# Compact 32x32 squares for the lower doublings of the delta chunks' inverse, and attention by tasks of both key heads in halves of the array

## The chip, the core and the metric

The kernel runs on one core of a Trainium2 chip. A core has a matrix engine (TensorE, PE in the rows, with PEld its weight loads), a vector engine (VectorE, DVE), a scalar engine (ScalarE, ACT), a general engine (GpSimd, POOL), and DMA queues, of which SyncE (SP) issues most. Each engine works through its own instructions in a fixed order and waits on semaphores for the others. The metric is the device time of one execution in microseconds (us), the median of several runs; lower is better.

## What is computed

Two transformer blocks over 1024 tokens of width 1024. The change lies in the mixers of the first block: attention with 8 query heads, 2 key heads of 64 wide and a sliding window of 128, and a gated delta rule with 4 heads of 128 wide in chunks.

```python
s = jnp.einsum('bnqhgd,bnkhd->bnhgqk', qb, kw) * scale     # block of 128 queries against itself and the block before
s = jnp.where(valid, s, -jnp.inf)
probs = softmax(concatenate([s, sink], -1))[..., :-1]
o = jnp.einsum('bnhgqk,bnkhd->bnqhgd', probs, vw)
...
L = where(strict, einsum('bhncd,bhnsd->bhncs', k_beta, k) * decay, 0.0)
T = triangular_solve(eye + L, eye, lower=True)             # the inverse that the doublings make
u = einsum('bhncs,bhnsd->bhncd', T, v_beta)
w = einsum('bhncs,bhnsd->bhncd', T, k_beta * exp(g)[..., None])
...                                                        # scan over chunks, then norm and gate
h = h + concatenate([attn_out, dn_out], -1) @ w_o
h = h + square(relu(rmsnorm(h) @ w_up)) @ w_down           # and a gate; then the second block
```

## The kernel before, in words

Tokens stand in two halves of 512 columns (`H`), features in tiles of 128 partitions. Projections are dense products of 128x128 weights with 512 columns, each as three products of split high and low parts (`acc`, L211 to L213); they take most of the time.

Between about 137 and 600 us of the profile `weave` interleaves three lanes of tasks with these dense products (`fills`). Its tasks are first attention, then the delta heads. Each round steps every live lane once (to its next `yield`) and adds `rate()` to a counter that releases one dense step (24 products) for each whole: `RA` at first, `RB` from `FA` finished attention tasks on, `R1` when all are done. Lane 0 takes only the first `FA` attention tasks and then starts on a delta head; the other lanes begin delta heads when all attention tasks are done. A scheduler then fixes the order on each engine from this program; the order doesn't change at run time. Each lane owns two PSUM tiles (`axps`, tags x0 to x2) and one SBUF tile for each role a to g, with two `tmp`.

Attention (`attn`) has 16 tasks, one for a block of 128 queries and one key head. A key head's 64 features lie in one half of the partitions, so its score products (L649, L651) use 64 rows of the array, and its value products (L679) write 64 columns. A task does two steps (`jj`) of two query heads: scores, mask (L654), softmax, transposes (L673), a copy of them (L675), values. The output tile `po` is taken at the start of the task and holds both steps until ACT copies it (L682).

A delta head (`delta`; 4 heads and 2 halves give 8 tasks) makes four 128x128 chunks at once and inverts the unit lower triangle of each by doublings: from a level's inverted blocks of side b the level makes blocks of side 2b. Levels 1 to 4 work on whole 128x128 matrices: `L` times the odd columns of `X` (L782), mask (L785), a DVE transpose of `X` within 32x32 blocks (L784), a second product (L789), subtraction (L790). Levels 5 and 6 already use squares of 32 and 64 (L807, L815). All products here are fp32, and the trace shows each product of this kind as two records, each with a weight load; the transposes by the array and the dense products are one record.

Of the kernel before, what the change touches and what calls it, by code (L numbers as in the profile page):

```python
# [19 lines left out]
NC = S // 128  # L20
# [33 lines left out]
RA, RB, R1, R5 = 0.1, 0.2, 0.35, 0.9  # L54
FA, POOL_AT = 10, 2
# [6 lines left out]
def block_kernel(ctx: ExitStack, tc: tile.TileContext, A):  # L62
# [12 lines left out]
    const.tile([128, 64], F32, name="pad")  # L75
# [82 lines left out]
    def mask(l):  # L158

        a = cst("masks")[:, l * 64:(l + 1) * 64].rearrange("p (n b) -> p n b", b=1 << l)  # L160
        return a.unsqueeze(1).to_broadcast([128, 4, 64 >> l, 1 << l])

# [357 lines left out]


# [112 lines left out]
    def attn(lane, qr, kr, vT, n, kv):  # L634
# [4 lines left out]
        r = slice(kv * 64, kv * 64 + 64)  # L639
        am = cst("amask")[:, 256 - w:256].unsqueeze(1).to_broadcast([128, 2, w])  # L640
        po = axps(lane)
        for jj in range(2):
            ps = axps(lane)
            p3 = ps[:, :2 * w].rearrange("p (j k) -> p j k", j=2)
            for i in range(2):
                q = qr[2 * jj + i][n // 4][r, cs(n % 4)]
                if n % 4 == 0:
                    for b, m in enumerate(blocks):
                        PE.matmul(p3[:, i, cs(b)], q, kr[m // 4][r, cs(m % 4)], start=True, stop=True)  # L649
                else:  # L650
# [5 lines left out]
            m, nm, den, s2 = sm(2, "am"), sm(2, "an"), sm(2, "ad"), sm(2, "as")  # L656
            sk = small("sinks", kv * 4 + 2 * jj, 2)
            V.tensor_reduce(m, e3, AX.X, ALU.max)
            V.tensor_tensor(m, m, sk, ALU.max)
            V.tensor_scalar(nm, m, -1.0, None, ALU.mult)  # L660
            for i in range(2):
                SC.activation(e3[:, i], e3[:, i], ACTF.Exp, bias=nm[:, i:i + 1], accum_out=s2[:, i:i + 1])
            V.tensor_tensor(den, sk, m, ALU.subtract)
# [3 lines left out]
            for i in range(2):  # L667
                V.tensor_scalar(e3[:, i], e3[:, i], den[:, i:i + 1], None, ALU.mult)
            yield
            pp = axps(lane)  # L670
            for q in range(nb):
                for i in range(2):
# [50 lines left out]
    def delta(lane, j, h, y, z):  # L723
# [697 lines left out]
```

## Time and profile before

| | |
|---|---|
| median of 3 runs | 2673.6 us |
| lowest and highest | 2668.96 and 2673.8 us |
| the profiled execution | 2670.03 us |
| its span, first to last instruction | 2667.9 us |
| PE busy | 2570.0 us, 96% of the span |
| DVE, ACT, POOL busy | 67%, 36%, 13% |

The profile is one execution. Its views give the busy time of each engine, in all and by stretch, groups of instructions of one line and shape, the engines' instructions in order of time, who waited for whom, and the chain of work that ended last. A matmul's duration includes its passage through the array and overlaps with the next, so what one costs PE is read from the distance between starts.

### The profile page before, as it was taken

The numbers are of one execution on the slowest core, as the hardware profiler recorded it, in microseconds if no ns is written. First come the engines' busy times: TensorE is split into PE (matmuls) and PEld (weight loads), VectorE is DVE, ScalarE is ACT, GpSimd is POOL, SyncE is SP. The second block draws the span as 40 slices with busy tenths as digits, with TensorE's granted clock in tenths as the row PEclk, the third lists the DMA queues.
The fourth block names the chain that finished last, engine by engine and source line by source line (L and its number), as shares of the span: only waits on it lengthen the run. The fifth ranks groups of instructions, "written<-read, shape, count | busy, mean of one in ns | idle before, by whom it ended". The sixth has DMA issues, their size and how long they took to land.

```text
span 2667.9 us, 34945 instructions
## 1 busy us (share of the span) xinstructions
PE 2570.0 (96%) x12814; PEld 2081.7 (78%) x12814; DVE 1794.8 (67%) x3289; ACT 971.1 (36%) x1568; POOL 356.9 (13%) x398
## 2 busy tenths in 40 slices
PE   6999999999899999999999999999988999999997
PEld 4766787877688888878877888888867888888886
DVE  8777789878987765465457643446589876654653
ACT  4477533314322245344333322222133222444441
POOL 5511112110000000000022343333200000000000
PEclk8999999999999999999999999999989999999998
DMA  5312111245644366445422411113455433665652
GB/s 199 95 52 68 41 37 52 94 148 183 206 157 133 127 229 227 166 152 196 151 78 69 160 56 40 44 34 105 152 181 191 155 131 131 214 210 195 220 195 77
DMA packets 161675, 357.00 MB, mean 134 GB/s; under 512 B 18272, under 2 KB 22752, under 8 KB 161504
## 3 DMA queue, kind: packets, MB, share of 16 engines
q1 hardware_dynamic: 156080, 345.84, 38.5%
q10 hardware_dynamic: 5424, 8.94, 1.0%
q8 instruction: 100, 1.64, 0.3%
q14 instruction: 71, 0.58, 0.1%
HBM read 282.35 MB, written 69.73 MB: 132 GB/s over the span
## 4 chain that ended last, share of the span: by engine, by line
PE 83%; DVE 9%; issue 4%; POOL 2%; DMA 1%; ACT 1%; POOLq 0%; SPq 0%; DVEq 0%; ACTq 0%
PE m L212 13%; PE m L213 13%; PE m L211 13%; PE x L213 10%; PE x L212 10%; PE x L211 10%; PE x L1196 1%; PE x L679 1%; PE x L789 1%; PE x L782 1%; DVE wl L192 1%; PE x L651 1%; DVE u L192 1%; PE x L1202 1%; PE x L673 1%
## 5 line engine op out<-in xcount | busy, mean ns | idle before, releaser
L211 PE MATMUL m<-u,wh 128*128 128x512 f32 x1668 | 671.8, 403 | 11.0 <-ACT wh L191 6.8
L213 PE MATMUL m<-u,wl 128*128 128x512 f32 x1668 | 665.4, 399 | 11.1 <-DVE wl L192 11.1
L212 PE MATMUL m<-u,wh 128*128 128x512 f32 x1668 | 666.9, 400 | 2.4 <-DVE u L192 1.2
L192 DVE TENSOR_TENSOR wl<-wr,wh 128x1024 fp32r<-128x1024 f32 (+2 forms) x265 | 328.0, 1238 | 296.5 <-ACT wh L191 283.0
L191 ACT CAST wh<-wr 128x1024 fp32r<-128x1024 f32 (+2 forms) x265 | 276.0, 1041 | 548.0 <-PE m L212 335.5
L213 PE MATMUL x<-u,wl 128*128 128x512 f32 x1020 | 397.9, 391 | 6.4 <-DVE wl L192 6.4
L212 PE MATMUL x<-u,wh 128*128 128x512 f32 x1020 | 398.5, 391 | 4.1 <-DVE u L192 4.1
L211 PE MATMUL x<-u,wh 128*128 128x512 f32 x1020 | 398.6, 392 | 2.4 <-ACT u L191 2.2
L211 PEld LDWEIGHTS m<-u,wh 128*128 128x128 f32 x1668 | 317.2, 190 | 80.7 <-ACT wh L191 7.3
L213 PEld LDWEIGHTS m<-u,wl 128*128 128x128 f32 x1668 | 317.2, 190 | 79.6 <-DVE wl L192 13.3
L212 PEld LDWEIGHTS m<-u,wh 128*128 128x128 f32 x1668 | 317.3, 190 | 73.6 <-issue 6.6
L213 PEld LDWEIGHTS x<-u,wl 128*128 128x128 f32 x1020 | 192.3, 189 | 47.6 <-DVE wl L192 7.7
L212 PEld LDWEIGHTS x<-u,wh 128*128 128x128 f32 x1020 | 192.1, 188 | 45.9 <-DVE u L192 5.4
L211 PEld LDWEIGHTS x<-u,wh 128*128 128x128 f32 x1020 | 192.2, 188 | 44.9 <-ACT u L191 3.5
L191 ACT CAST u<-f 128x512 fp32r<-128x512 f32 x198 | 122.1, 620 | 187.6 <-PE x L212 73.8
L192 DVE TENSOR_TENSOR u<-f,u 128x512 fp32r<-128x512 f32 x174 | 123.4, 709 | 95.0 <-PE x L212 50.9
L191 ACT CAST wh<-y 128x512 fp32r<-128x512 f32 x91 | 55.1, 621 | 218.9 <-PE x L212 131.3
L192 POOL TENSOR_TENSOR u<-f,u 128x512 fp32r<-128x512 f32 x24 | 35.6, 1481 | 609.2 <-ACT u L191 608.4
L192 DVE TENSOR_TENSOR u<-r,u 128x512 fp32r<-128x512 f32 x128 | 88.1, 688 | 5.8 <-ACT u L191 5.8
L191 ACT CAST u<-r 128x512 fp32r<-128x512 f32 x128 | 79.2, 619 | 11.6 <-DMA r<-hid 8.8
L192 DVE TENSOR_TENSOR wl<-y,wh 128x512 fp32r<-128x512 f32 x91 | 61.7, 682 | 0.0
L248 DVE TENSOR_TENSOR ac<-ac,sq 128x512 f32<-128x512 f32 x70 | 53.7, 767 | 9.5 <-ACT sq L247 8.7
(742 smaller groups left out, 3714.1 us busy)
## 6 DMA issues: line engine op xcount, KB each, us to landing
wr<-in_w_down SPq DMA_DIRECT2D x128, 512.0 KB, 4.0
wr<-in_w_in SPq DMA_DIRECT2D x75, 512.0 KB, 3.2
r<-hid SPq DMA_DIRECT2D x128, 256.0 KB, 4.0
f<-hid SPq DMA_DIRECT2D x128, 256.0 KB, 3.3
y<-in_w_up SPq DMA_DIRECT2D x85, 256.0 KB, 3.2
hid<-f SPq DMA_DIRECT2D x52, 256.0 KB, 2.0
wr<-in_w_up SPq DMA_DIRECT2D x20, 512.0 KB, 4.0
hid<-sq SPq DMA_DIRECT2D x32, 256.0 KB, 3.1
```

Source lines behind the costliest of these rows:

```text
L191: SC.copy(hi, src)
L192: eng.tensor_tensor(lo, src, hi.bitcast(F32), ALU.subtract)
L211: PE.matmul(ps, whi[:, s], xh, start=(first and k == 0), stop=False)
L212: PE.matmul(ps, whi[:, s], xl, start=False, stop=False)
L213: PE.matmul(ps, wlo[:, s], xh, start=False, stop=(last and k == len(x) - 1))
L248: V.tensor_tensor(a, a, sq, ALU.add)
L651: PE.matmul(p3[:, i], q, kr[n // 4][r, (n % 4 - 1) * 128:(n % 4 + 1) * 128], start=True, stop=True)
L673: PE.transpose(pp[:, cs(2 * q + i)], e3[:, i, cs(q)], ident)
L679: PE.matmul(po[r, jj * 256:jj * 256 + 256], vT[m // 4][:, b:b + 64], pT[:, q * 256:q * 256 + 256], start=(q == 0), stop=(q == nb - 1))
L782: PE.matmul(py[:, c * 64:c * 64 + 64], L[:, cs(c)], odd(X[:, cs(c)], l), start=True, stop=True)
L789: PE.matmul(pz[:, c * 64:c * 64 + 64], T[:, cs(c)], Y[:, c * 64:c * 64 + 64], start=True, stop=True)
L1196: PE.matmul(ps[:, c * 64:c * 64 + 64], k[:, cs(c)], odd(q[:, cs(c)], l), start=True, stop=True)
```

## The change

Delta heads: for levels 1 to 4 only the four 32x32 squares on the diagonal of each chunk are kept, side by side in a tile of 128 columns (`Xc`: partitions 32i to 32i+31 hold square i of all four chunks). A step is 16 products of one square with 16 columns (L817 and L824 of the new file, in place of L782 and L789), going round the four squares. The DVE operations on them have 128 or 64 columns in place of 512 or 256. The masks are made compact once at the start, by eight POOL copies. After level 4, POOL clears the full `X` and ACT copies the squares into it; level 5 reads the compact ones.

Attention: 8 tasks, one for each block of queries, with both key heads. A step takes two score tiles, one for each key head, and issues their products in turn on rows 0 to 63 and 64 to 127; the value products go in turn to the two column halves of one tile, which is now taken at the end of the step and copied and sent at once. `FA` goes from 10 of 16 tasks to 5 of 8, and `RA` and `RB` are doubled.

```diff
-RA, RB, R1, R5 = 0.1, 0.2, 0.35, 0.9
-FA, POOL_AT = 10, 2
+RA, RB, R1, R5 = 0.2, 0.4, 0.35, 0.9
+FA, POOL_AT = 5, 2
...
+    def dg(i):
+        return slice(32 * i, 32 * i + 32)
+
+    def cmask(l):
+        t = cmask4 if l == 4 else cmasks[:, l * 16:l * 16 + 16]
+        return t.unsqueeze(1).to_broadcast([128, 4, 16])
+
+    def cmasks_in():
+        for i in range(4):
+            m = cst("masks")[dg(i), :].rearrange("p (l n) -> p l n", l=5)[:, :, 16 * i:16 * i + 16]
+            G.tensor_copy(cmasks[dg(i), :].rearrange("p (l n) -> p l n", l=4), m[:, 0:4])
+            G.tensor_copy(cmask4[dg(i), :], m[:, 4])
...
+    cmasks_in()
...
-        r = slice(kv * 64, kv * 64 + 64)
+        rs = [slice(0, 64), slice(64, 128)]
         am = cst("amask")[:, 256 - w:256].unsqueeze(1).to_broadcast([128, 2, w])
-        po = axps(lane)
         for jj in range(2):
-            ps = axps(lane)
-            p3 = ps[:, :2 * w].rearrange("p (j k) -> p j k", j=2)
+            ps = [axps(lane), axps(lane)]
+            p3 = [p[:, :2 * w].rearrange("p (j k) -> p j k", j=2) for p in ps]
             for i in range(2):
-                q = qr[2 * jj + i][n // 4][r, cs(n % 4)]
+                q = qr[2 * jj + i][n // 4]
                 if n % 4 == 0:
                     for b, m in enumerate(blocks):
-                        PE.matmul(p3[:, i, cs(b)], q, kr[m // 4][r, cs(m % 4)], start=True, stop=True)
+                        for kv, r in enumerate(rs):
+                            PE.matmul(p3[kv][:, i, cs(b)], q[r, cs(n % 4)], kr[m // 4][r, cs(m % 4)], start=True, stop=True)
                 else:
-                    PE.matmul(p3[:, i], q, kr[n // 4][r, (n % 4 - 1) * 128:(n % 4 + 1) * 128], start=True, stop=True)
-            e = td("ab"[jj], lane)
-            e3 = e[:, :2 * w].rearrange("p (j k) -> p j k", j=2)
-            V.tensor_tensor(e3, p3, am, ALU.add)
+                    for kv, r in enumerate(rs):
+                        PE.matmul(p3[kv][:, i], q[r, cs(n % 4)], kr[n // 4][r, (n % 4 - 1) * 128:(n % 4 + 1) * 128], start=True, stop=True)
+            es = [td("ab"[kv], lane)[:, :2 * w].rearrange("p (j k) -> p j k", j=2) for kv in range(2)]
+            for kv in range(2):
+                V.tensor_tensor(es[kv], p3[kv], am, ALU.add)
             yield
...
+            for kv in range(2):
+                V.tensor_reduce(two(m, kv), es[kv], AX.X, ALU.max)
+            V.tensor_tensor(d2(m), d2(m), sk, ALU.max)
             V.tensor_scalar(nm, m, -1.0, None, ALU.mult)
...
+            for kv in range(2):
+                for i in range(2):
+                    k = 2 * kv + i
+                    SC.activation(es[kv][:, i], es[kv][:, i], ACTF.Exp, bias=nm[:, k:k + 1], accum_out=s2[:, k:k + 1])
...
-            for i in range(2):
-                V.tensor_scalar(e3[:, i], e3[:, i], den[:, i:i + 1], None, ALU.mult)
+            for kv in range(2):
+                V.tensor_tensor(es[kv], es[kv], two(den, kv).unsqueeze(2).to_broadcast([128, 2, w]), ALU.mult)
             yield
-            pp = axps(lane)
-            for q in range(nb):
-                for i in range(2):
-                    PE.transpose(pp[:, cs(2 * q + i)], e3[:, i, cs(q)], ident)
-            pT = td("tmp", lane)
-            SC.copy(pT[:, :2 * w], pp[:, :2 * w])
+            pT = []
+            for kv in range(2):
+                pp = axps(lane)
+                for q in range(nb):
+                    for i in range(2):
+                        PE.transpose(pp[:, cs(2 * q + i)], es[kv][:, i, cs(q)], ident)
+                t = td("tmp", lane)
+                SC.copy(t[:, :2 * w], pp[:, :2 * w])
+                pT.append(t)
             yield
+            po = axps(lane)
             for q, m in enumerate(blocks):
-                b = (m % 4) * 128 + kv * 64
-                PE.matmul(po[r, jj * 256:jj * 256 + 256], vT[m // 4][:, b:b + 64],
-                          pT[:, q * 256:q * 256 + 256], start=(q == 0), stop=(q == nb - 1))
-        f = td("tmp", lane)
-        SC.copy(f[r, :], po[r, :])
+                for kv, r in enumerate(rs):
+                    b = (m % 4) * 128 + kv * 64
+                    PE.matmul(po[r, 0:256], vT[m // 4][:, b:b + 64], pT[kv][:, q * 256:q * 256 + 256],
+                              start=(q == 0), stop=(q == nb - 1))
+            f = td("tmp", lane)[:, 0:256]
+            SC.copy(f, po[:, 0:256])
+            nc.sync.dma_start(
+                out=mix["d"][256 * jj:256 * jj + 256, cs(n)].rearrange("(i q) t -> q i t", q=128),
+                in_=f.rearrange("p (i t) -> p i t", i=2),
+            )
...
-        nc.sync.dma_start(
-            out=mix["d"][0:512, cs(n)].rearrange("(i q) t -> q i t", q=128)[r],
-            in_=f[r, :].rearrange("p (i t) -> p i t", i=4),
-        )
...
-        X = td("d", lane)
-        Y = td("a", lane)
-        G.tensor_copy(g4(X), b4(ident))
-        V.tensor_tensor(half4(Y, 0), odd(U, 0, 4), mask(0), ALU.mult)
-        V.tensor_tensor(odd(X, 0, 4), odd(X, 0, 4), half4(Y, 0), ALU.subtract)
...
+        Xc, Y = td("g", lane)[:, 0:128], td("a", lane)[:, 0:64]
+        y4 = lambda t: t[:, 0:64].rearrange("p (c n) -> p c n", c=4)
+        for i in range(4):
+            G.tensor_copy(Xc[dg(i), :].rearrange("p (c n) -> p c n", c=4), ident[dg(i), dg(i)].unsqueeze(1).to_broadcast([32, 4, 32]))
+        for i in range(4):
+            V.tensor_tensor(y4(Y)[dg(i)], g4(U)[dg(i), :, 32 * i + 1:32 * i + 32:2], cmask(0)[dg(i)], ALU.mult)
+        V.tensor_tensor(odd(Xc, 0), odd(Xc, 0), Y.unsqueeze(2), ALU.subtract)
         yield
+        blocks = [(c, dg(i), slice(c * 128 + 32 * i, c * 128 + 32 * i + 32), slice(c * 16, c * 16 + 16)) for c in range(4) for i in range(4)]
         for l in range(1, 5):
             py = axps(lane)
-            for c in range(4):
-                PE.matmul(py[:, c * 64:c * 64 + 64], L[:, cs(c)], odd(X[:, cs(c)], l), start=True, stop=True)
-            Y, T = td("a", lane), td("b", lane)
-            V.transpose(T, X)
-            V.tensor_tensor(half4(Y, l), half4(py, l), mask(l), ALU.mult)
+            for c, p, m, n in blocks:
+                PE.matmul(py[p, n], L[p, m], odd(Xc[p, dg(c)], l), start=True, stop=True)
+            Y, T = td("a", lane)[:, 0:64], td("b", lane)[:, 0:128]
+            V.transpose(T, Xc)
+            V.tensor_tensor(y4(Y), y4(py), cmask(l), ALU.mult)
             yield
             pz = axps(lane)
-            for c in range(4):
-                PE.matmul(pz[:, c * 64:c * 64 + 64], T[:, cs(c)], Y[:, c * 64:c * 64 + 64], start=True, stop=True)
-            V.tensor_tensor(odd(X, l, 4), odd(X, l, 4), half4(pz, l), ALU.subtract)
+            for c, p, m, n in blocks:
+                PE.matmul(pz[p, n], T[p, dg(c)], Y[p, n], start=True, stop=True)
+            V.tensor_tensor(odd(Xc, l), odd(Xc, l), pz[:, 0:64].rearrange("p (n b) -> p n b", b=1 << l), ALU.subtract)
             yield
+        X = td("d", lane)
+        G.memset(X, 0.0)
+        for i in range(4):
+            SC.copy(g4(X)[dg(i), :, dg(i)], Xc[dg(i), :].rearrange("p (c n) -> p c n", c=4))
...
             if l == 5:
-                V.transpose(T, X)
+                V.transpose(T[:, 0:128], Xc)
...
-                    PE.matmul(py[e, c * b:c * b + b], g4(L)[o, c, e], g4(X)[o, c, o], start=True, stop=True)
+                    x = Xc[o, dg(c)] if l == 5 else g4(X)[o, c, o]
+                    PE.matmul(py[e, c * b:c * b + b], g4(L)[o, c, e], x, start=True, stop=True)
...
-                    PE.matmul(pz[e, m], g4(T)[e, c, e], Y[e, m], start=True, stop=True)
+                    PE.matmul(pz[e, m], T[e, m] if l == 5 else g4(T)[e, c, e], Y[e, m], start=True, stop=True)
...
-        while over[0] < (FA if lane == 0 else 2 * NC):
+        while over[0] < (FA if lane == 0 else NC):
...
-    weave(tasks, fill, lambda: R1 if over[0] == 2 * NC else RB if over[0] >= FA else RA, few)
+    weave(tasks, fill, lambda: R1 if over[0] == NC else RB if over[0] >= FA else RA, few)
```

How PE's order changes in attention, where a task goes from its first step to its second. Before (L679 values, L651 scores of the second step, L673 transposes; x0 to x2 are the lanes' PSUM tiles, c, d, e and g hold queries and keys):

```order
L679 MATMUL x2_1222<-tmp2_1280,d1_231 64x256 x2
L651 MATMUL x2_1304<-c1_230,e0_228 128x256
L651 MATMUL x2_1304<-c1_230,g0_229 128x256
L212 MATMUL m_1758<-u_628,wh_1441 128x512
L213 MATMUL m_1758<-u_627,wl_1442 128x512
L211 MATMUL m_1758<-u_633,wh_1441 128x512
L212 MATMUL m_1758<-u_634,wh_1441 128x512
L673 MATMUL x0_1282<-consts0_90,b0_1232 128x128
```

In that place the new order has (L709 values, L671 scores, L700 transposes):

```order
L709 MATMUL x1_1326<-tmp1_1288,d1_240 64x256
L709 MATMUL x1_1326<-tmp1_1281,d1_240 64x256
L709 MATMUL x1_1326<-tmp1_1288,d1_240 64x256
L671 MATMUL x1_1334<-c1_239,e0_237 128x256
L671 MATMUL x1_1334<-c1_239,g0_238 128x256
L700 MATMUL x2_1344<-consts0_90,a2_1256 128x128 x4
L700 MATMUL x2_1351<-consts0_90,b2_1257 128x128 x4
L671 MATMUL x1_1335<-c1_239,e0_237 128x256
L671 MATMUL x1_1335<-c1_239,g0_238 128x256
L709 MATMUL x2_1436<-tmp2_1349,d1_240 64x256
L709 MATMUL x2_1436<-tmp2_1356,d1_240 64x256
```

The value products of the two key heads (tmp1_1281 and tmp1_1288) alternate. The score products of the second step do not: both of one head (x1_1334), then another lane's transposes, then both of the other head (x1_1335).

PE in the delta heads, two lanes in their doublings. Before (L789 and L782 are the two steps of a level, a, b, c and d the lanes' matrices):

```order
L211 MATMUL m_3446<-u_950,wh_3435 128x512
L212 MATMUL m_3446<-u_951,wh_3435 128x512
L789 MATMUL x2_3108<-a2_3064,b2_3065 128x64 x4
L789 MATMUL x1_3149<-a1_3104,b1_3105 128x64 x4
L213 MATMUL m_3446<-u_950,wl_3436 128x512
L211 MATMUL m_3446<-u_956,wh_3435 128x512
L212 MATMUL m_3446<-u_957,wh_3435 128x512
L213 MATMUL m_3446<-u_956,wl_3436 128x512
L782 MATMUL x2_3155<-d2_2948,c2_2946 128x64 x4
L782 MATMUL x1_3164<-d1_2879,c1_2877 128x64 x4
```

Now, in the same part:

```order
L227 MATMUL m_3264<-u_941,wh_3253 128x512
L817 MATMUL x1_3169<-g1_2759,c1_2757 32x16 x16
L228 MATMUL m_3264<-u_942,wh_3253 128x512
L229 MATMUL m_3264<-u_941,wl_3254 128x512
L824 MATMUL x2_3190<-a2_3157,b2_3158 32x16 x16
L227 MATMUL m_3264<-u_947,wh_3253 128x512
L228 MATMUL m_3264<-u_948,wh_3253 128x512
L894 MATMUL x0_3208<-g0_3166,a0_3039 128x128
L824 MATMUL x1_3212<-a1_3186,b1_3187 32x16 x16
L817 MATMUL x2_3230<-g2_2825,c2_2823 32x16 x16
```

Sixteen small products stand where four stood, between the same dense ones; some runs of two lanes touch, as before.

## Rows read from the trace of the kernel before

**Rows 1.** The page: the span, and each engine's busy time, share and instructions.
```profile
span 2667.9 us, 34945 instructions
PE 2570.0 (96%) x12814; PEld 2081.7 (78%) x12814; DVE 1794.8 (67%) x3289; ACT 971.1 (36%) x1568; POOL 356.9 (13%) x398
```

**Rows 2.** The page: 40 slices of the span, busy tenths and granted clock.
```profile
PE   6999999999899999999999999999988999999997
...
PEclk8999999999999999999999999999989999999998
```

**Rows 3.** Busy us by stretch: PE, PEld, DVE, ACT, POOL, granted clock, DMA.
```profile
137.00:313.00 176.00, 174.94 (x901) 120.07 (x899) 130.60 (x384) 121.10 (x282) 22.99 (x36) 1.00 0.18 57
313.00:600.00 287.00, 276.15 (x2037) 231.35 (x2038) 242.24 (x623) 90.15 (x135) 54.92 (x56) 1.00 0.23 79
```

**Rows 4.** Chain that ended last, shares by line: 137 to 313, then 313 to 600.
```profile
by line: PE x L679 16.8%; PE x L651 14.1%; PE m L212 12.9%; PE m L213 12.4%; PE m L211 11.7%; PE x L673 8.1%; PE x L649 2.9%; PE x L789 2.0%; PE x L782 2.0%; DVE b L668 1.9%; DVE am L658 1.7%; DVE y L713 1.5%; DVE wl L192 1.3%; DVE b L654 1
by line: PE m L212 9.7%; PE m L211 9.6%; PE m L213 9.5%; PE x L789 8.0%; PE x L782 8.0%; DVE y L713 3.2%; DVE w L220 2.6%; issue 2.5%; PE x L854 2.4%; PE x L849 2.3%; PE x L864 2.2%; DVE wl L192 2.2%; PE x L851 2.1%; PE x L840 2.0%; PE x L8
```

**Rows 5.** PE in order of time, a doubling step: start us, us, what.
```profile
270.66 0.39 PE L211 MATMUL m<-u,wh 128*128 128x512 f32 x1
270.88 1.00 PE L782 MATMUL x<-d,c 128*128 128x64 f32 x8
...
272.01 0.39 PE L213 MATMUL m<-u,wl 128*128 128x512 f32 x1
```

**Rows 6.** PE in order of time, 32x32 squares of level 5.
```profile
286.34 0.40 PE L211 MATMUL m<-u,wh 128*128 128x512 f32 x1
286.66 0.44 PE L807 MATMUL x<-d,c 32*32 32x32 f32 x16
...
287.37 0.40 PE L213 MATMUL m<-u,wl 128*128 128x512 f32 x1
```

**Rows 7.** Groups by line and shape, 137 to 600: busy us, mean ns.
```profile
L807 PE MATMUL x<-d,c 32*32 32x32 f32 x128 | 3.8, 194 | 0.0
```

**Rows 8.** PE in order of time: quarters of the columns, and whole-array products.
```profile
306.71 0.43 PE L232 MATMUL x<-tmp,ones 128*32 128x128 f32 x8
...
313.48 1.05 PE L756 MATMUL x<-y 128*128 128x128 f32 x8
```

**Rows 9.** Groups by shape, DVE, 137 to 600.
```profile
L784 DVE STREAM_TRANSPOSE b<-d 128x512 f32<-128x512 f32 x32 | 22.5, 703 | 0.1
L785 DVE TENSOR_TENSOR a<-x,consts 128x256 f32<-128x256 f32 x32 | 13.3, 416 | 7.2 <-PE x L782 7.2
L234 DVE STREAM_TRANSPOSE b<-x 128x256 f32<-128x256 f32 x8 | 3.6, 444 | 5.2 <-PE x L232 5.2
```

**Rows 10.** The output copy of attention: its wait (us, times, longest) and group.
```profile
ACT tmp L682 <- PE x L679: 12.3, 8, 2.0
L682 ACT COPY tmp<-x 64x512 f32<-64x512 f32 x16 | 9.2, 575 | 12.4 <-PE x L679 12.3
```

**Rows 11.** PE in order of time, half-array products of attention.
```profile
280.17 0.38 PE L679 MATMUL x<-tmp,g 128*64 128x256 f32 x1
...
281.06 0.70 PE L651 MATMUL x<-e,e 64*128 64x256 f32 x2
...
282.12 1.08 PE L679 MATMUL x<-tmp,g 128*64 128x256 f32 x4
283.13 0.70 PE L651 MATMUL x<-e,e 64*128 64x256 f32 x2
```

**Rows 12.** POOL at the start, its small copies, and the constants' DMA.
```profile
18.45 2.09 POOL L245 TENSOR_TENSOR sq<-y 128x512 f32<-128x512 f32 x1 [2.49 <-DVE ac L248]
43.24 0.65 POOL L706 COPY x<-tails 128x3 f32<-128x3 f32 x1 [1.28 <-DVE f L269]
L706 POOL COPY x<-tails 128x3 f32<-128x3 f32 x20 | 6.2, 312 | 27.7 <-DVE ha L221 27.7
consts<-in_consts ACTq DMA_DIRECT2D x1, 436.0 KB, 6.7
```

More of the change, by code (lines that the diff above doesn't have):

```diff
@@ L73, in block_kernel @@
     ps_ = ctx.enter_context(tc.tile_pool(name="ps", bufs=1))
-    const.tile([128, 64], F32, name="pad")
+    cmasks = const.tile([128, 64], F32, name="cmasks")
     psm = ctx.enter_context(tc.tile_pool(name="psm", bufs=2, space=bass.MemoryType.PSUM))
@@ L161, in mask @@
         return a.unsqueeze(1).to_broadcast([128, 4, 64 >> l, 1 << l])
+    cmask4 = const.tile([128, 16], F32, name="cmask4")
+    def dg(i):
[8 more added lines that the diff above has]
+            G.tensor_copy(cmask4[dg(i), :], m[:, 4])
     def b4(ap, n=4):
@@ L632, in block_kernel, with attn @@
     V.tensor_scalar(neg, dec[:, 0:32], -1.0, None, ALU.mult)
-    def attn(lane, qr, kr, vT, n, kv):
+    def attn(lane, qr, kr, vT, n):
         blocks = [n] if n == 0 else [n - 1, n]
@@ L656, in attn @@
[L656 to L659, printed above, removed]
-            V.tensor_scalar(nm, m, -1.0, None, ALU.mult)
-            for i in range(2):
-                SC.activation(e3[:, i], e3[:, i], ACTF.Exp, bias=nm[:, i:i + 1], accum_out=s2[:, i:i + 1])
-            V.tensor_tensor(den, sk, m, ALU.subtract)
+                        for kv, r in enumerate(rs):
+                            PE.matmul(p3[kv][:, i, cs(b)], q[r, cs(n % 4)], kr[m // 4][r, cs(m % 4)], start=True, stop=True)
+                else:
+                    for kv, r in enumerate(rs):
+                        PE.matmul(p3[kv][:, i], q[r, cs(n % 4)], kr[n // 4][r, (n % 4 - 1) * 128:(n % 4 + 1) * 128], start=True, stop=True)
@@ new lines, in attn @@
+            es = [td("ab"[kv], lane)[:, :2 * w].rearrange("p (j k) -> p j k", j=2) for kv in range(2)]
+            for kv in range(2):
+                V.tensor_tensor(es[kv], p3[kv], am, ALU.add)
+            yield
+            m, nm, den, s2 = [sm(4, t) for t in ("am", "an", "ad", "as")]
+            two = lambda t, kv: t[:, 2 * kv:2 * kv + 2]
+            sk = small("sinks", 0, 8).rearrange("p (v j) -> p v j", v=2)[:, :, 2 * jj:2 * jj + 2]
+            d2 = lambda t: t.rearrange("p (v j) -> p v j", v=2)
@@ new lines, in attn @@
+            for kv in range(2):
+                V.tensor_reduce(two(m, kv), es[kv], AX.X, ALU.max)
+            V.tensor_tensor(d2(m), d2(m), sk, ALU.max)
+            V.tensor_scalar(nm, m, -1.0, None, ALU.mult)
+            for kv in range(2):
+                for i in range(2):
+                    k = 2 * kv + i
+                    SC.activation(es[kv][:, i], es[kv][:, i], ACTF.Exp, bias=nm[:, k:k + 1], accum_out=s2[:, k:k + 1])
+            V.tensor_tensor(d2(den), sk, d2(m), ALU.subtract)
@@ L666, in attn @@
             V.reciprocal(den, den)
-            for i in range(2):
-                V.tensor_scalar(e3[:, i], e3[:, i], den[:, i:i + 1], None, ALU.mult)
+            for kv in range(2):
+                V.tensor_tensor(es[kv], es[kv], two(den, kv).unsqueeze(2).to_broadcast([128, 2, w]), ALU.mult)
             yield
-            pp = axps(lane)
-            for q in range(nb):
-                for i in range(2):
-                    PE.transpose(pp[:, cs(2 * q + i)], e3[:, i, cs(q)], ident)
-            pT = td("tmp", lane)
-            SC.copy(pT[:, :2 * w], pp[:, :2 * w])
+            pT = []
[7 more added lines that the diff above has]
+                pT.append(t)
             yield
+            po = axps(lane)
             for q, m in enumerate(blocks):
-                b = (m % 4) * 128 + kv * 64
-                PE.matmul(po[r, jj * 256:jj * 256 + 256], vT[m // 4][:, b:b + 64],
-                          pT[:, q * 256:q * 256 + 256], start=(q == 0), stop=(q == nb - 1))
-        f = td("tmp", lane)
-        SC.copy(f[r, :], po[r, :])
+                for kv, r in enumerate(rs):
[8 more added lines that the diff above has]
+            )
         mix["done"].update((n // 4, i) for i in range(4))
-        nc.sync.dma_start(
-            out=mix["d"][0:512, cs(n)].rearrange("(i q) t -> q i t", q=128)[r],
-            in_=f[r, :].rearrange("p (i t) -> p i t", i=4),
-        )
     tails = const.tile([128, 36], F32, name="tails")
@@ L881, in block_kernel, with attn_task @@
     over = [0]
-    def attn_task(lane, n, kv):
-        yield from attn(lane, *qkv, n, kv)
+    def attn_task(lane, n):
+        yield from attn(lane, *qkv, n)
         over[0] += 1
     def delta_task(lane, jh):
-        while over[0] < (FA if lane == 0 else 2 * NC):
+        while over[0] < (FA if lane == 0 else NC):
             yield
@@ L906, in block_kernel @@
     fill = fills()
-    tasks = [lambda lane, n=n, kv=kv: attn_task(lane, n, kv) for n in range(NC) for kv in range(2)]
+    tasks = [lambda lane, n=n: attn_task(lane, n) for n in range(NC)]
     few = tasks[FA:]
     tasks += [lambda lane, jh=jh: delta_task(lane, jh) for jh in order]
-    weave(tasks, fill, lambda: R1 if over[0] == 2 * NC else RB if over[0] >= FA else RA, few)
+    weave(tasks, fill, lambda: R1 if over[0] == NC else RB if over[0] >= FA else RA, few)
     run(out_last(mix, range(4, 8), wb, 2, hm, 1))
```

## The prediction

> **What bounds the kernel now.** I read the page first: TensorE (PE) is busy 96% of the span, and no other engine passes 67% [rows 1]. Next the 40 slices: the change touches only the stretch in which attention and the delta heads are woven into the projections, slices 3 to 9, and there PE stands at 9 with its clock granted in full, 2.4 GHz [rows 2]. Then the table of that stretch: in 137 to 313 us (attention, with the first delta head) PE is busy 174.9 of 176 us, DVE 130.6, ACT 121.1; in 313 to 600 us (the other delta heads) PE 276.2 of 287, DVE 242.2, ACT 90.2 [rows 3]. The chain of waits says the same: in the first half L679, L651 and L673, the products of attention, hold 39% of the chain, and in the second L782 and L789, the doublings, hold 16% [rows 4]. So the weave is bound by the order of PE, and an edit is worth what it takes from or adds to PE's queue. Busy time overstates a product (matmuls overlap), so I price products by the distance from one start to the next.
>
> **The doublings.** Before, each of 8 heads does 4 levels with two steps each: 64 steps of 4 products, which the trace shows as 8 records, since an fp32 product is two. One step stands between dense products at 270.66: from the L211 ahead of it to the second dense product behind it, at 272.01, are 1.35 us, of which the two dense products take 0.23 each; the step costs 0.89 [rows 5]. That is 64 x 0.89 = 57.0 us.
> After, a step is 16 products of a 32x32 square with 16 columns, 32 records. The nearest rows are the 32x32 products of L807. Sixteen of them between dense products cost 287.37 - 286.34 - 0.46 = 0.57 us; one lasts 0.19 by its group and all last 0.44, so starts are (0.44 - 0.19)/15 = 17 ns apart and the rest, 0.57 - 0.27 = 0.30, is the price of turning the array to small squares and back [rows 6, 7]. L807 uses two squares in turn, so one square takes a new product every 34 ns; the new code goes round four. If four overlap, a record costs 34/4 = 8.5 ns; if only two do, 17; if none, 34. That four parts of the array run together is shown for quarters of its columns: eight L232 products of 128 columns are busy 0.43 us together, while eight of that width on the whole array (L756) need 1.05 [rows 8]. I take 8.5 and keep 17 for the range. The instruction order has 61 runs of such products (some steps of two heads stand together), so after: 2048 x 0.0085 + 61 x 0.30 = 17.4 + 18.3 = 35.7 us, a gain of 21 (at 17 ns: 53.1, a gain of 4).
> Here the Trainium skill speaks against the change: "TensorEngine Tiling (Array Packing)", section Gotcha 1: PSUM Pressure, says that different row tiles can't access one PSUM bank at the same time, and all four squares write one tile. By that a record would cost 34 ns, which is the first rival below with its 2689 us; but L807 too has two row groups writing one tile, and its starts are 17 ns apart.
>
> **DVE, ACT and POOL in the delta heads.** The 40 transposes shrink from 512 to 128 columns: 0.70 us at 512 and 0.44 at 256, so about 0.31, 15 us less; the 64 masks and subtractions shrink from 256 columns, 0.42 us, to 64, for which I estimate 0.2, 14 us less [rows 9]. PE is idle for only 11 of the 287 us in 313 to 600 [rows 3], so shorter DVE steps can give back no more than that; I count them at nothing and keep the 11 for the lower end. Added are four ACT copies a head, at most 0.58 us each by L682, 19 us in all [rows 10], and on POOL a memset and four small copies for one copy. Level 5 reads the compact squares, and the copies are needed only at level 6; ACT has 197 us free in that stretch and POOL 232 [rows 3], so nothing. Without that cover the ACT copies would cost up to those 19 us.
>
> **Attention.** The same 72 score products, 60 value products and 120 transposes remain; the two key heads now use opposite halves of the array and can run side by side where they stand side by side in the order. Four value records last 1.08 us and one about 0.39, so a record takes 0.23 and a product of 256 columns 0.46 [rows 11]. In the order the value products alternate: of 14 blocks of four, six are unbroken (two steps saved each) and eight are split by another product (one saved), and two blocks of two save one each: 22 x 0.46 = 10.1 us. The scores mostly do not: beyond the first steps both products of one head stand together and the other head's follow later. I count nine places where halves of 256 columns meet and six of 128 columns (0.22): 9 x 0.46 + 6 x 0.22 = 5.4 us. Runs of half-array products fall from 64 to 48; by the starts at 281.06, 282.12 and 283.13 a run costs about 0.12 over its records [rows 11], so 2 us. In all 17.5 us; if the halves did not overlap at all, 2.
> DVE has half as many small operations and two products with a broadcast for four scalings; about 17 us less work, counted at nothing.
> **A new wait.** A lane has two PSUM tiles. The value output now takes its tile only at the end of a step, and the next step's second score tile is that same tile, so it waits until ACT has copied the output. Behind it in PE's queue stand transposes and value products of the other lanes. Eight tasks, once each. The copy of before follows its products by 12.3 us in 8 waits, 1.5 us, and lasts 0.58 [rows 10]: up to 2 us each, 16 in all. But in five of the eight places the order puts four or more other products ahead of the waiting one; three follow at once and can pay 2 us each. I take 5 us.
> **The numbers in front.** With FA at 5 of 8 tasks, and rates doubled for half as many steps, projections come as before: the order has 820 dense products from the first score to the last head's output before, 802 now, and 18 that move behind it. Nothing.
> **The start.** Eight mask copies now stand in POOL's queue between two squarings of the first norm, and DVE's sum, the rope and the projections' scaling wait behind them. Their input, the second block of constants, lands 6.7 us after its issue and is issued ahead of the first norm, so I take it as there by then. A small copy takes 0.31 on the mean and 0.65 in this stage [rows 12], so eight take 2.5 to 5.2 us, against 2.49 us in which POOL is idle there: 0 to 2.7, I take 1.
>
> **The sum.** The profiled execution took 2670.0 us (span 2667.9 and 2.1 around it), near the median of 2673.6 and inside the three runs. 2670.0 - 21 - 17.5 + 5 + 1 = 2637.5; I say 2637.
>
> **The rivals.** *Squares do not overlap*: the four share a bank or a port, and a record costs 34 ns: 69.6 + 18.3 = 87.9 us, 31 more than before, and the time is 2637.5 + 21 + 31 = 2689, slower. It decides at the record time where the doublings lose what the rest gains, 11.5 us: (57 + 11.5 - 18.3)/2048 = 24.5 ns. Against it stand L807 and L232 [rows 6, 8].
> *A floor of starts*: PE hands out small products no faster than halfway between L807's 17 ns and a square's own 34, 25.5 ns; the doublings then cost 52.2 + 18.3 = 70.5, 13.5 more than before, and the time is 2637.5 + 21 + 13.5 = 2672. L807's 17 ns on two squares speaks against it [rows 6, 7]. The Trainium skill, "TensorE: Matmul & The Clock Gate", section Wait — 56ns, not 53.3ns?, has a floor of about 25 ns between the starts of matmuls however small they are; by it this rival would be an estimated 2671, and the trace does not agree with it as far as two squares go.
> *Attention moves to its vector chain*: three lanes with tasks twice as wide, DVE and ACT each at 69 to 74% of that half already [rows 3], so that PE's saved time turns into waits for softmax: attention gives nothing, 2637.5 + 17.5 - 5 = 2650, and if squares also overlap by two only, 2667. For it: longer exponentials in a row on ACT; against it: both engines have less to do than before.
> *PE's idle time closes too*: DVE's shorter steps give back the 11 us: 2626.
>
> **How the numbers follow.** Forecast (2630 to 2646): 0.50. Attention's gain lost, or squares by two (2646 to 2664): 0.23. Idle time closes as well (below 2630): 0.12. The floor or the sum of several losses, ending within 0.2%: 0.08. Squares in a row, or waits near their 16 us with them: 0.07. A difference under 0.2%, 5 us, can't be told from none. Range: 2616 leaves out little below, and 2665 leaves out the two last cases and part of the second. Faster 0.85, same 0.08, slower 0.07.
>
> **What would show it.** In the profile after: 32 records of a doubling step in about 0.45 us with starts near 8 ns; the score and value products of the two heads starting in pairs; the second score tile's wait for the ACT copy, 5 us in total; the attention half shorter by 12 us for the same dense products and the delta half by 21. PE idle over 15 us more in attention, or record starts over 24 ns, would prove me wrong.

## The result, and the profile after

The changed kernel takes 2641.6 us (median of 4 runs, 2640.1 to 2642.95) where the kernel before took 2672.0 on the same chip (4 runs, 2669.0 to 2673.8): a ratio of 0.9887, interval 0.987 to 0.9904, 30 us less. The forecast was 2637, its range 2616 to 2665. The profiled execution has a span of 2641.2 us against 2667.9 [rows 1]. The page of after, engines and then slices:

```profile
span 2641.2 us, 37995 instructions
PE 2536.3 (96%) x14350; PEld 2047.5 (78%) x14350; DVE 1761.3 (67%) x3201; ACT 973.0 (37%) x1584; POOL 379.2 (14%) x438
...
PE   6999999998999999999999999999988999999997
...
PEclk8999999999999999999999999999999999999998
```

PE is still at 96%, and the slices read as before [rows 2], so what moved must be looked for inside the weave. After's lines are 16 to 40 higher in number: the doublings L782 and L789 are L817 and L824 now, the scores L649 and L651 are L668 and L671, the values L679 are L709.

PE in order of time, one doubling step between dense products in after (start us, us, what), the answer to [rows 5]:

```profile
497.86 0.40 PE L229 MATMUL m<-u,wl 128*128 128x512 f32 x1
498.18 0.44 PE L824 MATMUL x<-a,b 32*32 32x16 f32 x32
...
498.89 0.39 PE L228 MATMUL m<-u,wh 128*128 128x512 f32 x1
```

By the measure that gave 0.89 us before, the step costs 498.89 - 497.86 - 0.46 = 0.57 us. Its 32 records last 0.44 us together and 0.18 each, so starts are 0.26/31 = 8.4 ns apart.

The same view in attention, the answer to [rows 11]: scores of the two key heads start at the same instant, and eight value records take the 1.08 us that four took.

```profile
180.45 0.48 PE L671 MATMUL x<-e,e 64*128 64x256 f32 x1
180.45 0.48 PE L671 MATMUL x<-e,g 64*128 64x256 f32 x1
...
181.50 1.08 PE L709 MATMUL x<-tmp,d 128*64 128x256 f32 x8
```

**A ledger of the weave.** From the first score to the start of the 817th dense product behind it, before needs 451.1 us and after 420.6, for the same work but for ten records of the last head's small products, which in before stand behind that point. I gave each PE record the time from its start to the next record's start, less the time in which no product ran, and added these up by line:

| us | before | after | |
|---|---|---|---|
| lower doublings | 53.7 | 25.2 | -28.5 |
| other products of the delta heads | 82.4 | 89.5 | +7.1 |
| levels 5 and 6 | 16.7 | 15.8 | -0.9 |
| dense products | 212.7 | 211.6 | -1.1 |
| scores | 31.8 | 26.4 | -5.4 |
| value products | 30.5 | 20.8 | -9.7 |
| transposes of attention | 12.1 | 14.0 | +1.9 |
| no product running | 11.1 | 17.3 | +6.2 |
| all | 451.1 | 420.6 | -30.5 |

The price of turning the array to squares and back lies partly on a step's neighbours, so the first two rows belong together: -21.4. The rows of after also hold 10.2 us at half clock (below), which cost about half of that.

What PE waited for (us in total, times, longest), in after from 137 to 560, then in before from 137 to 595:

```profile
PE x L778 <- POOL tmp L777: 8.0, 12, 2.0
PE x L437 <- POOL tmp L433: 3.5, 5, 1.3
PE x L700 <- DVE a L693: 1.5, 1, 1.5
```
```profile
PE x L748 <- POOL tmp L747: 4.3, 9, 0.9
PE x L421 <- POOL tmp L417: 2.4, 4, 1.2
```

L777 (L747) is a head's decay mask and L433 (L417) the norm's scaling of its output, both on POOL; PE's waits for the two grew from 6.7 to 11.5 us. Neither list has a wait of a score product for ACT, and after's has one wait for softmax, 1.5 us.

Busy us by stretch in after (PE, PEld, DVE, ACT, POOL, granted clock, DMA), the answer to [rows 3]:

```profile
137.00:313.00 176.00, 170.29 (x1630) 120.65 (x1629) 136.24 (x352) 119.23 (x279) 37.85 (x54) 0.98 0.19 58
...
276.00:282.00 6.00, 4.60 (x103) 3.48 (x101) 5.59 (x24) 3.79 (x8) 0.74 (x4) 1.00 0.01 3
282.00:289.00 7.00, 6.98 (x91) 5.08 (x92) 2.93 (x13) 0.00 (x0) 0.00 (x0) 0.51 0.24 77
...
401.50:405.00 3.50, 3.50 (x48) 3.24 (x47) 3.40 (x8) 0.60 (x1) 1.37 (x2) 0.51 0.38 136
...
620.00:627.00 7.00, 6.29 (x23) 4.85 (x16) 4.70 (x16) 1.48 (x2) 0.00 (x0) 0.51 0.49 154
...
1130.00:1150.00 20.00, 14.24 (x48) 11.02 (x49) 11.85 (x16) 8.32 (x14) 2.80 (x2) 0.74 0.53 160
```

Before had the full clock all through the weave [rows 3]; after has two stretches at 1.2 GHz in it, 6.8 and 3.4 us. Each is the profile of one execution. In the first one PE had stood still for 1.4 of the 6 us ahead. At 1.2 GHz a dense product takes nearly twice as long, PE in order of time (0.43 us from start to start, 0.23 at 2.4 GHz):

```profile
286.62 0.63 PE L229 MATMUL m<-u,wl 128*128 128x512 f32 x1
287.05 0.63 PE L227 MATMUL m<-u,wh 128*128 128x512 f32 x1
```

Behind the weave the same work meets more of it too: 0.74 over 1130 to 1150, where before has 0.91 over the same stretch:

```profile
1158.00:1178.00 20.00, 14.11 (x55) 11.07 (x56) 13.02 (x17) 9.30 (x15) 2.80 (x2) 0.91 0.46 159
```

Of the 30.5 us that the weave gives, 26.7 are left at the end of the span.

### The profile page after: what moved, and what is told of

It is laid out like the page before. It is cut to its first block, busy times and chain, and to the rows that moved or that the text cites. A ratio compares the mean times of both kernels' runs of the same rounds, so it can differ in the third digit from the quotient of the medians.

```text
span 2641.2 us, 37995 instructions
## 1 busy us (share of the span) xinstructions
PE 2536.3 (96%) x14350; PEld 2047.5 (78%) x14350; DVE 1761.3 (67%) x3201; ACT 973.0 (37%) x1584; POOL 379.2 (14%) x438
## 4 chain that ended last, share of the span: by engine, by line
PE 65%; issue 3%; DVE 3%; POOL 1%; DMA 1%; ACT 1%; POOLq 0%; SPq 0%; DVEq 0%; ACTq 0%
PE x L229 10%; PE x L228 10%; PE x L227 10%; PE m L227 10%; PE m L228 10%; PE m L229 10%; PE x L1236 1%; PE x L1242 1%; POOL u L208 0%; DVE wl L208 0%; PE x L1221 0%; PE x L1259 0%; PE x L1273 0%; PE x L1275 0%; DVE u L208 0%
## 5 line engine op out<-in xcount | busy, mean ns | idle before, releaser
L264 DVE TENSOR_TENSOR ac<-ac,sq 128x512 f32<-128x512 f32 x70 | 53.7, 766 | 10.5 <-ACT sq L263 8.7
```

The source lines that it names most:

```text
L264: V.tensor_tensor(a, a, sq, ALU.add)
```

## The experiments

Every run, with its median and its ratio to the kernel before on the same chip; the edits below are made to the changed kernel, but for before_dve.

| run | us | ratio, 95% interval |
|---|---|---|
| the change | 2641.6 | 0.9887 (0.9870 to 0.9904) |
| squares_only | 2659.8 | 0.9942 (0.9927 to 0.9957) |
| attn_only | 2663.8 | 0.9955 (0.9939 to 0.9971) |
| square_by_square | 2675.9 | 1.0006 (0.9996 to 1.0015) |
| same_half | 2648.3 | 0.9903 (0.9887 to 0.9920) |
| gates_apart | 2637.4 | 0.9868 (0.9852 to 0.9885) |
| head_out_dve | 2626.7 | 0.9827 (0.9812 to 0.9842) |
| both_waits | 2627.0 | 0.9830 (0.9813 to 0.9847) |
| before_dve | 2672.4 | 0.9993 (0.9984 to 1.0002) |
| masks_late | 2638.5 | 0.9870 (0.9855 to 0.9885) |
| busy_gaps | 2638.3 | 0.9870 (0.9854 to 0.9887) |
| dve_late | 2626.9 | 0.9824 (0.9809 to 0.9839) |
| dve_late_busy | 2630.0 | 0.9833 (0.9818 to 0.9847) |

**The two parts alone.** The first has before's `attn`, rates and tasks, the second before's doublings:

```
-    def attn(lane, qr, kr, vT, n):              # squares_only
+    def attn(lane, qr, kr, vT, n, kv):
-            for c, p, m, n in blocks:           # attn_only
-                PE.matmul(py[p, n], L[p, m], odd(Xc[p, dg(c)], l), ...)
+            for c in range(4):
+                PE.matmul(py[:, c * 64:c * 64 + 64], L[:, cs(c)], odd(X[:, cs(c)], l), ...)
```

> Before's attention, with before's rates and its task counts, and the new squares in the delta heads. Theory of the sum (the two halves of the change add up): 21 us less than before by the forecast's price of 0.30 us for a run plus 8.5 ns a record, up to 27 us less by what the two lines give back from start to start in the trace of the changed kernel: 2645 to 2651 us. Rival (the squares only bring forward waits on the vector side, and attention carried the gain): under 10 us less, 2662 or above. If the two new stretches at half clock at 282 and 402 us of the changed kernel belong to the squares, PE's granted clock falls to 0.5 somewhere inside the weave here too; if they belong to attention, it stays at 1.0.

> The new attention with its rates and task counts, and before's doublings in full 128x128 products. Theory of the sum: 12.5 us less than before with the new wait of 5 us paid, 15 to 17.5 without it: 2654 to 2660 us, value and score products together 15 us shorter from start to start. Rival (the attention half moves to its vector chain, with wider tasks in three lanes): 0 to 5 us less, 2667 to 2672, and PE idle over 15 us more between 137 us and the last value product. No stretch at half clock inside the weave if those belong to the squares.

The squares alone give 15.5 us (11.5 to 19.5), less than the theory's 21 and more than the rival's 10. Their ledger has the doublings at 24.8 us (-28.9), the heads' other products at 88.7 (+6.3) and PE without work for 15.4 (+4.3); the weave is 16.4 shorter. Attention alone gives 12 us (8 to 16), just under the theory's 12.5: values -10.7 and scores -5.4, but 17.0 us without work (+5.9) and 13.7 us at half clock, so its weave is only 6.5 shorter. Together that is 27.5, the change's 30 within the intervals: the halves add up. The waits for the two POOL steps grow with either half, in squares_only first, then in attn_only (6.7 us before):

```profile
PE x L766 <- POOL tmp L765: 6.1, 11, 1.3
PE x L437 <- POOL tmp L433: 3.9, 7, 1.0
```
```profile
PE x L760 <- POOL tmp L759: 7.3, 12, 2.0
PE x L421 <- POOL tmp L417: 4.7, 6, 1.5
```

attn_only adds nothing to POOL in the heads and has 12.0 us of them, so the steps that the change adds on POOL aren't needed for that growth. The half clock is in both weaves (3.4 us in squares_only), and before_dve below, with neither part, has 10.2 us of it in its own: it belongs to neither part alone.

**Do the squares overlap?**

```
-  blocks = [... for c in range(4) for i in range(4)]
+  blocks = [... for i in range(4) for c in range(4)]
```

> The changed kernel, but the 16 products of a step go square by square (all four chunks on one 32x32 square, then the next square) in place of going round the four squares. Theory (the doublings are cheap because four squares run at once, and one square takes a record every 34 ns): a step's 32 records span about 1.05 us in place of 0.26, and 64 steps add about 50 us, 2690, some of it less where the records fill a wait: 2675 to 2692. Rival (a record is cheap because it has 16 columns, in whatever square): 0.26 us a step as before and 2641, within 3 us.

The whole gain is gone: 1.2% slower than the change, 32 us. The same kind of step, PE in order of time:

```profile
524.87 0.40 PE L229 MATMUL m<-u,wl 128*128 128x512 f32 x1
525.20 0.88 PE L824 MATMUL x<-a,b 32*32 32x16 f32 x32
...
526.34 0.39 PE L228 MATMUL m<-u,wh 128*128 128x512 f32 x1
```

The records take 0.88 us, not 0.44. One square takes a record every 32 ns, but where the order turns to the next square the two run side by side for a while, so the span is 0.70 us and not the 1.05 I expected. The doublings' lines rise by 27 us and the weave by 37; in it the clock stands at half for 44 us against 10, which by the dense products' 0.43 for 0.23 us is an estimated 16 of the 37. That too comes with the order: its ten executions were granted 0.977 to 0.980, the change's four 0.982 to 0.984. The rival falls by the row above, which is at full clock.

**Does attention gain by its halves?**

```
-        rs = [slice(0, 64), slice(64, 128)]
+        rs = [slice(0, 64), slice(0, 64)]
...
-            for q, m in enumerate(blocks):
-                for kv, r in enumerate(rs):
-                    PE.matmul(po[r, 0:256], ...)
+            for kv, r in enumerate(rs):
+                for q, m in enumerate(blocks):
+                    PE.matmul(po[r, kv * 256:kv * 256 + 256], ...)
```

> The changed kernel, but both key heads use the upper half of the array: scores of both heads are of the first head's rows, and both heads' value products write rows 0 to 63 of the output tile, side by side in columns (so the second head's scores are left out and the first head's are computed twice). The same number of products of the same size, tasks, rates and vector work. Theory (attention gains because two heads' products run at once in opposite halves): the value products lose 9.7 us and the scores 5.3, so 2656 us, 2651 to 2660. Rival (the gain comes from half as many and wider tasks, fewer changes of the array's form and less vector work): 2641 to 2645.

The same block of eight value records as at 181.50 above:

```profile
181.43 1.94 PE L709 MATMUL x<-tmp,d 128*64 128x256 f32 x8
```

1.94 us for 1.08. Over the weave values cost 28.8 us (+8.0) and scores 31.3 (+4.9), and it is 10.2 us longer, which is the theory. But the time is only 4 to 7 us above the change's, between theory and rival, and the intervals overlap: the time alone decides nothing. The mean granted clock tells them apart: in the profiled executions it is 0.986 of 2644.5 us against 0.982 of 2641.2, so the clock took 37 us here and 47.5 there. At the same clock, 0.984, two executions of same_half took 2650.2 and 2651.7 us and two of the change 2640.1 and 2642.1: some 10 us, the theory's lower edge.

**PE's waits for POOL.** gates_apart writes the decay masks to empty tiles, head_out_dve moves one product from POOL to DVE, both_waits does both, and before_dve makes the second edit in the kernel before:

```
-            gt = td("tmp", lane, F32R)
+            gt = td("cd"[i], lane, F32R)
...
-        G.tensor_tensor(g4(o), g4(o), col4(r.unsqueeze(2)), ALU.mult)
+        V.tensor_tensor(g4(o), g4(o), col4(r.unsqueeze(2)), ALU.mult)
```

> The changed kernel, but the two decay masks that POOL makes at a head's start go to the tiles c and d of their lane, which stand empty then, in place of the two tmp tiles from which the squares of the norm are still being read: POOL no longer waits for the sums of the squares. Theory (what the change lost of its gain went into new waits of PE for the vector side, and into the clock that falls behind them): the seven gaps of 0.5 to 2.0 us before L778, 6.5 us in all, close, and at least one of the two stretches at half clock in the weave, behind such gaps at 282 and 402 us, goes with them: 2630 to 2636 us. Rival (the gap only moves to what is late next, POOL's other work or DVE): PE's idle time in the weave stays, 2639 to 2643.

> The changed kernel, but the scaling by which each head's output is normed, 128x512 on POOL (about 1.3 us), stands on DVE (about 0.75 by products of that size). Theory (PE waits for this one step at the end of every head, in gaps of 0.5 to 2.0 us before L437, three of them in the weave with 3.1 us and some six behind it with 6.7): about half of the gaps closes, 3 to 5 us less: 2636 to 2639. Rival (DVE, at 67% of the span, hands the wait on to its other steps): 2641 or above.

> Both edits at once, the masks in c and d and the norm's scaling on DVE. Theory (the two waits lie at different places and add up): 2626 to 2633 us. Rival (once PE waits for neither, the next step on DVE is as late): no faster than the better of the two alone.

> The kernel before, with the norm's scaling of each head's output on DVE in place of POOL, the edit that made the changed kernel 15 us faster. Theory (the change shortened the work that lies beside this step, so most of the 10 us that it gives inside the weave is a wait that the change made): 6 us from the layer behind it, where both kernels are the same, and up to 3 in the weave, where PE stood 2.7 us before this step: 2662 to 2667. Rival (the step was as late before): 13 to 17 us less, 2655 to 2660.

PE's waits in gates_apart, 137 to 560:

```profile
PE x L437 <- POOL tmp L433: 5.1, 6, 2.0
PE x L800 <- DVE b L789: 2.8, 2, 2.3
PE x L700 <- DVE bb L770: 1.6, 1, 1.6
```

The wait for L777 is gone from the list and others stand in its place: 16.3 us without work after 17.3. That is the rival. The stretch at 282 is gone, as the theory had it, but the one near 402 is twice as long; the time of 2637.4 can't be told from the change's. The scaling and PE's wait for it, in the change and then in head_out_dve:

```profile
L433 POOL TENSOR_TENSOR tmp<-tmp,hr x8: 1038/1039/1479, 338.2 to 560.9; 128x512 f32<-128x512 f32 x8
...
  PE x L437: 11.2, 12
```
```profile
L433 DVE TENSOR_TENSOR tmp<-tmp,hr x8: 677/688/1762, 334.5 to 550.6; 128x512 f32<-128x512 f32 x8
...
  PE x L437: 3.6, 7
```

It takes 0.69 us, where POOL took 1.04, and PE waits 3.6 us for it over the whole span, where it had waited 11.2. The kernel takes 2626.7 us, 15 less than the change; no run is faster by more than its interval. I expected 3 to 5. The weave gives 8.3 (3.4 of it idle time, and 3.4 us at half clock in place of 10.2), the heads of the next layer 6.6, between the 5500th and the 6500th dense product. both_waits lies in its theory's range, but is no faster than the scaling alone, which is its rival.

In the kernel before the same edit gives nothing, where the theory had 7 to 12 us and the rival 13 to 17: neither. By the starts of the same dense products in the two profiles, the next layer does give 6.6 us and the weave 3.3, as the theory had it. But 12.5 are lost in the 130 us behind the weave, where the last head's scaling is late (PE waits 3.4 us for it from 603 on) and the clock falls, and 3 at the start, ahead of the edit:

```profile
598.00:605.50 7.50, 4.83 (x22) 3.65 (x20) 6.29 (x22) 1.68 (x2) 0.00 (x0) 1.00 0.60 206
605.50:613.00 7.50, 4.79 (x14) 3.51 (x15) 3.28 (x5) 1.66 (x3) 0.00 (x0) 0.54 0.52 175
```

That execution took 2677.3 us, 5 above the median of the run's eleven, so it overstates the loss. The clocks of all executions say more. The share of the clock that isn't granted, times the time, is 44 us for the change (0.983 on the mean of four) and 37 for head_out_dve (0.986): an estimated 7 of the 15 us are the clock. In the kernel before it is 45 us with the edit (0.983, eleven) and 41 without it (0.985, fifteen). At equal clock the edit would thus be worth some 8 us in the changed kernel and 5 in the one before. That the difference between those two is the change's longer waits isn't shown.

**The start and the clock.** masks_late moves the eight mask copies; busy_gaps sets useless products into three gaps (the new `warm` argument holds the last two squares, in three norms); dve_late is head_out_dve with masks_late, dve_late_busy all three:

```
-    cmasks_in()                      # ahead of the gates' weights
     qkv = attn_in()
+    cmasks_in()                      # masks_late
...
         ps = axps(lane)              # sums(), busy_gaps
+        for x in warm:
+            PE.matmul(ps, ones, x, start=True, stop=True)
```

> The changed kernel, but POOL's eight mask copies stand behind the input projections of attention in place of the first norm. Theory (they cost 2.6 us at dense product 100, but by product 300, at 115 us, the two kernels are level again, since what follows waits for something else): no change, 2640 to 2643, and the stretches at half clock in the weave stand where they did, which also tells whether they come back from run to run. Rival (the start's delay is carried to the end, as the prediction had it with 1 us): 1 to 2.6 us less.

> The changed kernel with work added: in three of the twelve norms, those at whose sums PE stands still for 2.0 to 4.7 us (at 618, 1423 and 2624 us), two products of the last squares with the ones matrix, 128x512 each, about 0.9 us, which nobody reads, stand ahead of the sums. They fall in time in which PE waits. Theory (the clock falls to half behind such gaps, and this is what takes back some of the change's gain behind the weave): the stretches at half clock at 620 and 1425 us, 6.8 us each, shrink or go, and the kernel is 2 to 6 us faster with six products more: 2635 to 2639. Rival (the clock falls for another reason, or the gaps left suffice): the stretches stay, and the time is 2641 to 2644.

> The changed kernel with the norm's scaling of each head's output on DVE and the mask copies behind attention's input projections, the two edits that were faster alone (by 15 and 3 us). Theory (they lie at different places and add up): 2622 to 2625. Rival (what the late masks gave came from where the clock fell, behind the weave, and not from the start): 2626 to 2629, as with the scaling alone.

> The kernel with both edits, and the six idle products in the three gaps. Theory of the clock: 2 to 6 us below the one without them, 2617 to 2622. Rival: within 2 us of it.

masks_late: at the 400th dense product it is 1.7 us ahead of the change, and that stays through the weave, whose length is the same (420.8 us) with the half clock at the same places, 280 to 287 and 400 to 403; in busy_gaps it stands at 270 and 400, 3.4 us each. The 1.7 us can't be put down to the copies: head_out_dve, which leaves them in place, is 1.4 ahead at that product, and dve_late, which moves them, 2.2 behind head_out_dve. Behind the weave the stretch at 620 is missing, and there masks_late gains 2.8 more. Its interval overlaps the change's, and dve_late adds nothing to head_out_dve, so no price of the copies is shown.

Busy us by stretch at the two gaps in question: the second one in the change (the first is shown above), then both in busy_gaps, then the first in masks_late:

```profile
1425.50:1432.50 7.00, 4.83 (x24) 2.95 (x25) 6.15 (x14) 2.16 (x3) 0.00 (x0) 0.51 0.32 98
```
```profile
616.00:623.00 7.00, 6.00 (x31) 4.14 (x30) 6.59 (x18) 1.22 (x2) 0.00 (x0) 1.00 0.42 121
...
1421.00:1428.00 7.00, 6.34 (x37) 4.29 (x38) 6.62 (x19) 1.89 (x3) 0.00 (x0) 1.00 0.33 109
```
```profile
618.00:625.00 7.00, 5.99 (x31) 4.40 (x31) 5.28 (x17) 1.35 (x2) 0.00 (x0) 1.00 0.58 175
```

Both stretches at half clock are gone, in dve_late_busy too. For the one at 1425 PE's standing still ahead of it was what made it fall: it stands in all twelve profiles without the added products and in neither of the two with them. For the one at 620 that isn't shown: masks_late has the full clock there without them, and so has before, where PE stands still for 2.0 us ahead of the same norm, as it does in the change. The time hardly moves: 3 us less here, 3 more there, neither beyond its interval. Without the stretch at 620 the dense products behind it come 2.8 us earlier, without the one at 1425 another 1.4.

## Why the prediction was right, and where not

*The squares.* Right: 8.4 ns a record against a forecast of 8.5, a step of 0.57 us against 0.27 + 0.30, and -21.4 for the first two rows of the ledger against -21. That the two agree so well is in part luck: the forecast's 57.0 and 35.7 are 53.7 and, with the neighbours' 7.1, 32.3 in the ledger, 3.3 and 3.4 lower, and the second holds some of the half clock. Squares do not wait for each other, and no floor stood in the way. Two rules of the Trainium skill had spoken against it. "TensorEngine Tiling (Array Packing)", Gotcha 1: PSUM Pressure, keeps row tiles off one PSUM bank at a time; four row groups write one tile here at 8.4 ns, so the measurement decides against it for this form. The floor of about 25 ns in "TensorE: Matmul & The Clock Gate", section Wait — 56ns, not 53.3ns?, holds at most on one square, where square_by_square shows 32 ns.

*Attention.* The terms of value and score products were right: -9.7 against a forecast of -10.1, -5.4 against -5.4, and same_half shows that the halves make them. The 2 us for fewer changes of the array did not come; the transposes between cost 1.9 more. The term was -17.5 and measures -13.2.

*The new wait* was a miss: 5 us forecast, 0 found; at none of the eight places is a score late for ACT.

*DVE, ACT and POOL counted at nothing* was the wrong step, on the other side from where I looked. I kept up to 11 us for idle time that would close. It grew instead, by 6.2, and 4.8 of that are PE's waits for the POOL steps at a head's start and end. The likely cause is that these are still there while the PE work beside them is shorter: the waits grow with either half of the change alone. It isn't proven, since gates_apart takes the first wait away and its weave has other waits in its place. The two waits of the list stood before as well, at 6.7 us, so the trace held the place.

*The clock* was in no term. In the weave its 10.2 us at half cost an estimated 5. Behind it 3.6 us are given back, where the work is the same and the granted clock is lower. Over whole executions the change's four lose 44 us to the clock by the mean granted share, and the kernel before, by its 42 in the experiments (0.984 to 0.986 by chip), 39 to 42.

*The sum.* The weave's gain, 30.5, is 3 us short of the forecast's 33.5, but that is the rest of larger misses that cancel: 4.3 in attention and 6.2 of idle time against the 5 us wait that never came and 2.4 in the other rows. So the closeness of the total is in part luck. With the 3.6 behind the weave and the start's 1 us, of which the profile has 0.2, it makes 2637.5 + 3 + 3.6 - 0.8 = 2643.3; the profiled execution took 2642.95, and the median is 1.4 lower.

*The rivals.* Squares in a row or at a floor: excluded. Attention on its vector chain: no, since attention gives 13.2 us and PE waits 1.5 for softmax. Idle time closing: the opposite. Neither of the two signs of being wrong came.

## What to carry over

Price products by the distance between starts, and small squares by how many different ones stand next to each other in the order: four in turn ran nearly four times as fast as one. When the bound engine's work shrinks, list its present waits first, and look for the steps beside that work that don't shrink with it: here the waits for two of them grew from 6.7 to 11.5 us. On differences under half a per cent compare the mean granted clock of all executions before believing a mechanism: here it moved the time by as much as a term did.

## What I had not expected of the hardware

The clock also falls where PE never stands still. In square_by_square, busy us by stretch:

```profile
550.00:557.00 7.00, 7.00 (x166) 5.81 (x167) 3.30 (x11) 0.00 (x0) 0.00 (x0) 1.00 0.34 113
557.00:571.00 14.00, 14.00 (x123) 11.31 (x119) 6.48 (x16) 2.59 (x6) 0.00 (x0) 0.51 0.19 66
```

PE is busy for all of the 7 us ahead, and then runs at 1.2 GHz for 14; what it did there were squares, one at a time, and 128x128 products, with four dense products among them. So PE's busy share doesn't tell whether the clock will hold.
